# Rows of the split-weight buffers 1032 elements apart in place of 1024

## The chip, the cores and the metric

The kernel runs on one core of one Trainium2 chip. The metric is the device time of one execution, in microseconds (us). A time before of 1797.07 us is the median of three runs.

## What is computed

Two layers of an encoder block on 512 tokens of 1024 features, all in float32:

```
for l in range(2):
    x = x + 0.5 * swiglu(rms_norm(x, ffn1_norm[l]), ffn1_w_gate[l], ffn1_w_up[l], ffn1_w_down[l])
    p = rms_norm(x, mix_norm[l]) @ w_in[l]
    attn = mla_group(p[..., :672], ...)        # latent attention, 8 heads, chunk mask
    conv = conv_group(p[..., 672:], ...)       # gated causal depthwise convolution, 31 taps
    x = x + concatenate([attn, conv]) @ w_out[l]
    x = x + 0.5 * swiglu(rms_norm(x, ffn2_norm[l]), ffn2_w_gate[l], ffn2_w_up[l], ffn2_w_down[l])
    x = rms_norm(x, post_norm[l])

swiglu(x, g, u, d) = (silu(x @ g) * (x @ u)) @ d      # 1024 -> 2816 -> 1024
```

Nearly all of the arithmetic is in the matrix products with weights: four feed-forward blocks (two in each layer), the input projection and the output projection.

## The kernel before

**Split products.** Every float32 operand is split in two parts that TensorE takes in its float32r format: a high part, made by a cast on ScalarE, and a low part, the rest, made by a subtraction on VectorE. A product then is three (`mm3`, lines 170 to 172): high weights by high activations, high weights by low activations, low weights by high activations, all summed in PSUM. The weights are the stationary operand and the activations, features by tokens, the moving one.

**Weights.** A block of weights comes in by DMA as 128 rows of up to 1024 float32, into a tile `raw` (3 buffers) or, in the feed-forward blocks, also `fr` (4 buffers). `load_w` (lines 147 to 159) and `split_into` (lines 257 to 263) make the high part `wh` (line 151 or 260) and the low part `wl` (line 157 or 262). Each of `wh` and `wl` has 4 buffers, taken in turn, in the pool `w`. Some low parts are made by a DMA that adds the weights to their negated high part: into `ls` (`subtracted`, lines 405 and 406), or into `wl` for part of the output projection. A column block of 128 elements, 512 bytes in a row, is the stationary operand of one product.

**Activations.** The split activations lie in a ring `r` of 35 buffers of 512 elements, or, in the feed-forward blocks, also in `xj` (six buffers that hold high and low part side by side) and `xs`. In the mixing block between them some lie in `m`, a tile of a pool that is opened for that block.

**Feed-forward blocks.** The 22 column blocks of 128 hidden features are taken in pairs, in chunks (`CHUNKS`). The first two pairs of a block are computed plainly, with 512 columns (tokens) a product. For the others a fast scheme of seven block products in place of eight is used (`pair`), with operands combined by additions on VectorE. There the products have 256 columns, apart from those of `product_joined` (lines 389 and 390), where high and low activations of `xj` stream together as 512 columns against the high weights, and the high ones alone as 256 against the low weights. `down` does the same scheme for the middle chunks of the down projection, with 256 columns; the first and last chunk are computed plainly with 512.

**Order of the work.** The program is written in a fixed order and scheduled by a tool that orders each engine's instructions by priority and places tiles in memory. `issue_after` sets some orders by hand. Each pool is a stretch of memory whose tiles follow one another in the order in which their tags first appear:

```
cpool = ctx.enter_context(tc.tile_pool(name="const", bufs=1))
ring = ctx.enter_context(tc.tile_pool(name="ring", bufs=RING))
tmps = ctx.enter_context(tc.tile_pool(name="tmps", bufs=5))
wpool = ctx.enter_context(tc.tile_pool(name="w", bufs=4))
small = ctx.enter_context(tc.tile_pool(name="small", bufs=2))
```

In `w` the order is `raw`, `wh`, `wl`. The pools of the feed-forward and mixing blocks (`f`, with `fr`, `xj`, `xs`, `ls`; `k`, with `m`) are opened after `small` and lie behind it.

Of the kernel before, what the change touches and what calls it, by code (L numbers as in the profile page):

```python
# [7 lines left out]
FP = mybir.dt.float32  # L8
FR = mybir.dt.float32r
# [6 lines left out]
P = 128  # L16
# [15 lines left out]
NF = F // P  # L32
EPS = 1e-6
WC = 1024
HS = S // 2
RING = 35
WIDE = 6
# [41 lines left out]
def encoder_kernel(ctx: ExitStack, tc: tile.TileContext, xT, consts, vecs, rgain, wgu1, wd1, wdq1,  # L79
# [6 lines left out]
    wpool = ctx.enter_context(tc.tile_pool(name="w", bufs=4))  # L86
# [4 lines left out]
    def nm(s):  # L91
        uid[0] += 1
        return f"{s}{uid[0]}"
# [7 lines left out]
    def bank():  # L101
        return psum.tile([P, S], FP, tag="ps", name=nm("ps"))
# [44 lines left out]
    def load_w(src, w, kind=""):  # L147
        raw = wpool.tile([P, WC], FP, tag="raw", name=nm("raw"), bufs=3)
        nc.sync.dma_start(out=raw[:, :w], in_=src)
        hi = wpool.tile([P, WC], FR, tag="wh", name=nm("wh"))  # L150
        order["cast"] = A.copy(hi[:, :w], raw[:, :w]).ins  # L151
        lo = low()
        if kind == "sum":
            A.activation(lo[:, :w], raw[:, :w], AF.Copy, scale=-1.0)
            G.dma_start(out=lo[:, :w], in_=src, accum_op=ALU.add)
            return hi, lo
        (G if kind in POOLW.split() else V).tensor_tensor(lo[:, :w], raw[:, :w], hi[:, :w].bitcast(FP),  # L157
                                                          ALU.subtract)
        return hi, lo

    def low():
        return wpool.tile([P, WC], FR, tag="wl", name=nm("wl"))

    order = {}

# [3 lines left out]
    def mm3(o, lh, ll, rh, rl, first, last, free=False):  # L169
        T.matmul(o, lh, rh, start=first, stop=False, skip_group_check=free)  # L170
        T.matmul(o, lh, rl, start=False, stop=False, skip_group_check=free)  # L171
        order["mm"] = T.matmul(o, ll, rh, start=False, stop=last, skip_group_check=free).ins  # L172
        return order["mm"]
# [74 lines left out]
    def groups(srcs, rhs, ws=None):  # L248

        ws = ws or [load_w(src, WC) for src in srcs]  # L250
        os = [bank() for _ in srcs]
        for ks in (range(KD - 1), range(KD - 1, KD)):
            for o, w in zip(os, ws):
                group(o, w, rhs, ks, KD)
        return os

    def split_into(q, src, w=WC):

        hi = wpool.tile([P, WC], FR, tag="wh", name=nm("wh"))
        A.copy(hi[:, :w], src[:, :w])  # L260
        lo = low()
        order["lo"] = V.tensor_tensor(lo[:, :w], src[:, :w], hi[:, :w].bitcast(FP), ALU.subtract).ins  # L262
        return hi, lo
# [5 lines left out]
    def ffn_body(fpool, l, gx, norm, wgu, wd, wdq, gain, done, w0, halved):  # L269
# [52 lines left out]
        def operands(R):  # L322

            def joined(src):
                both = fpool.tile([P, 2, S], FR, tag="xj", name=nm("xj"), bufs=WIDE)
                A.copy(both[:, :, 0:HS], src)
                V.tensor_tensor(both[:, :, HS:S], src, both[:, :, 0:HS].bitcast(FP), ALU.subtract)
                return both
# [13 lines left out]
            for i in range(2):  # L342
                e, o = wide(quarter()), wide(quarter())
                for j in range(2):
                    for par, t in ((0, e), (1, o)):
                        m = 4 * i + 2 * j + par
                        V.scalar_tensor_tensor(t[:, j], x[:, m, :], gain[:, m:m + 1], R, ALU.mult, ALU.mult)
                        yield
                b11, b12, b21, b22 = (v[:, :, h * HS:(h + 1) * HS] for v in (e, o) for h in range(2))
                for n, src in (("b11", b11), ("b21", b21)):  # L350
# [21 lines left out]
        def product(o, w, n, start, stop):  # L372
            with tc.issue_after(order["pe"]):
                for gu in range(2):
                    for k in range(4):
                        hi, lo = X[n][k // 2]
                        t = slice(k % 2 * HS, (k % 2 + 1) * HS)
                        c = slice(gu * 512 + k * P, gu * 512 + (k + 1) * P)
                        last = mm3(o[:, gu * HS:(gu + 1) * HS], w[0][:, c], w[1][:, c], hi[:, t], lo[:, t],
                                   start and gu == 0 and k == 0, stop and k == 3, True)  # L380
            order["pe"] = last

        def product_joined(os, w, n, start):
            with tc.issue_after(order["pe"]):
                for gu, o in enumerate(os):
                    for k in range(4):
                        both = X[n][k // 2][:, k % 2]
                        c = slice(gu * 512 + k * P, gu * 512 + (k + 1) * P)
                        T.matmul(o, w[0][:, c], both, start=start and k == 0, stop=False, skip_group_check=True)  # L389
                        last = T.matmul(o[:, 0:HS], w[1][:, c], both[:, 0:HS], start=False, stop=k == 3,  # L390
                                        skip_group_check=True).ins
# [10 lines left out]
        def subtracted(w, src, n=WC):  # L402

            lo = fpool.tile([P, WC], FR, tag="ls", name=nm("ls"), bufs=2)
            A.activation(lo[:, :n], src[:, :n], AF.Copy, scale=-1.0)  # L405
            G.dma_start(out=lo[:, :n], in_=w, accum_op=ALU.add)  # L406
            return lo

        def summed(w, src, n=WC, lo=None):

            lo = subtracted(w, src, n) if lo is None else lo
            hi = wpool.tile([P, WC], FR, tag="wh", name=nm("wh"))
            A.copy(hi[:, :n], src[:, :n])
            return hi, lo

        def pair(p, quartered):

            a11, a12, a21, a22, s3 = quarters(wgu[l, p], WC, p == CHUNKS[0][1])
            bx, by, bz = bank(), (bank(), bank()), (bank(), bank())
            product(bx, split_into("a11", a11), "b11", True, True)  # L420
            a = copied(tmp(), bx)
            product_joined(by, summed(wgu[l, p, 1], a12), "b21", True)
            with after("first"):
                V.tensor_tensor(s3, a11, a21, ALU.add)
# [4 lines left out]
            for c, main, rest in parts(by):  # L429
                V.tensor_tensor(a[:, c], a[:, c], main, ALU.add)  # L430
                V.tensor_tensor(a[:, c], a[:, c], rest, ALU.add)
                if c.start == 0:
                    A.activation(s[:, 0:HS], a[:, 0:HS], AF.Silu)
            V.tensor_tensor(s[:, 0:HS], s[:, 0:HS], a[:, HS:S], ALU.mult)
            product(bx, split_into("s2", a11), "t2", False, True)
            r2 = wide(fpool.tile([P, WC], FP, tag="e", name=nm("e"), bufs=1))
            copied(r2[:, 0], bx)
            product_joined(bz, split_into("s3", s3), "t3", True)
            d = [copied(tmp(), o) for o in bz]
            for t in d:  # L440
# [3 lines left out]
            for t, (c, _, _) in zip(d, parts(bz)):  # L444
                order["first"] = V.tensor_tensor(r2[:, 1, c], t[:, 0:HS], r2[:, 1, c], ALU.subtract).ins
            product_joined(bz, summed(wgu[l, p, 3], a22), "t4", False)
            for c, main, rest in parts(bz):
                V.tensor_tensor(r2[:, 0, c], main, r2[:, 0, c], ALU.subtract)
# [89 lines left out]
        for p0, p1 in CHUNKS:  # L538
# [3 lines left out]
            for p in range(p0, p1):  # L542
                if p == 0:
                    os = []
                    for r in range(2):
                        ws = w0[2 * r:2 * r + 2] if w0 else [load_w(wgu[l, p, 2 * r + q], WC) for q in range(2)]
                        os.append([bank(), bank()])
                        if w0 and not r:
                            plain_first(os[r], ws)
                        elif w0:  # L550
                            plain(os[r][:1], ws, range(KD))
                            plain([None] + os[r][1:], ws, range(KD // 2))
                            with tc.issue_after(order["mm"]):
                                norm()
                            with after("sums"):
                                plain([None] + os[r][1:], ws, range(KD // 2, KD))
                        else:
                            plain(os[r], ws, range(KD - 1))
                            plain(os[r], ws, range(KD - 1, KD))
                            if not w0:  # L560
                                R = norm()
                    if not w0:
                        scaled(os, R)
                elif p < CHUNKS[0][1]:
                    for r in range(2):
                        ws = [load_w(wgu[l, p, 2 * r + q], WC) for q in range(2)]
                        o = [bank(), bank()]
                        if w0 and not r:
                            with tc.issue_after(order["mm"]):
                                plain(o[:1], ws, KS[:KD // 4])  # L570
                            with tc.issue_after(order["mm"]):
                                R = norm()
                            with after("spread"):
                                plain(o[:1], ws, KS[KD // 4:])
                                plain([None] + o[1:], ws, range(KD))
                            scaled(os, R)
                        else:
                            plain(o, ws, range(KD))
                        advance(8)
                        act.append(plain_out(o, R))  # L580
                else:
                    order.setdefault("pe", order["mm"])
                    act += pair(p, p0 > 0 and not last)
# [9 lines left out]
            for m in range(halved if last else KD):  # L593
                if m in ahead:
                    pd, w = ahead[m]
# [438 lines left out]
    class Finish:  # L1034
# [54 lines left out]
        def __call__(self):  # L1089
# [4 lines left out]
            for t in range(NT):  # L1094
# [8 lines left out]
    st = Stats()  # L1103
    f = gained(0, "g1", gx, first_gain)
    f(0)
    w0 = [tuple(wpool.tile([P, WC], t, tag=tag, name=nm(tag), bufs=n)
                for t, tag, n in ((FP, "raw", 3), (FR, "wh", 4), (FR, "wl", 4))) for _ in range(2)]

    def half_w(q, gu):
        raw, hi, lo = (v[:, gu * 512:(gu + 1) * 512] for v in w0[q])  # L1110
# [12 lines left out]
    w0 = [w[1:] for w in w0]  # L1123
# [172 lines left out]
```

## Time and profile before

| | |
|---|---|
| median of 3 runs | 1797.07 us (1794.69 to 1797.32) |
| the profiled execution | 1794.2 us |
| its span in the trace | 1792.4 us |
| TensorE products busy | 1778.5 us (99%) |
| TensorE weight loads busy | 1579.1 us (88%) |
| VectorE busy | 1493.5 us (83%) |
| ScalarE busy | 1093.8 us (61%) |
| GpSimd busy | 382.1 us (21%) |
| moved by DMA | 228.28 MB, 127 GB/s in the mean |

In the profile, PE is TensorE's matrix products and PEld its loads of stationary operands, which run beside the products; DVE is VectorE, ACT ScalarE, POOL GpSimd, SP the engine that issues most DMAs. A row of a grouped view names the line, the engine, the operation, the tile written, the tiles read, the shape and the count; after the bar stand the busy time, the mean duration in ns and the engine's idle time before such instructions, with what ended it. Products are pipelined, so the mean duration of one is longer than the time from its start to the next one's. A row of the timeline begins with start and duration in us.

### The profile page before, as it was taken

What the parts mean: (1) busy time and instruction counts of PE and PEld (TensorE: products, weight loads), DVE (VectorE), ACT (ScalarE), POOL (GpSimd) and SP (SyncE); (2) the same over time, 40 slices, a digit from 0 to 9 for tenths busy, and PEclk for the clock granted to TensorE, in tenths of its full rate; (3) what the DMA queues carried; (4) which work ended last, traced back from release to release, by engine and by line L of the source; (5) the groups of instructions that cost most, each with busy time, mean ns of one, the idle gap of its engine ahead of it and who ended that gap; (6) DMA issues with size and microseconds to landing.
All of it is one profiled execution on the core that took longest, in us unless ns stands there. A gap on an engine that the chain in (4) does not pass through costs nothing.

```text
span 1792.4 us, 29441 instructions
## 1 busy us (share of the span) xinstructions
PE 1778.5 (99%) x11430; PEld 1579.1 (88%) x11430; DVE 1493.5 (83%) x2309; ACT 1093.8 (61%) x1699; POOL 382.1 (21%) x313
## 2 busy tenths in 40 slices
PE   9999999999999999999999999999999999999998
PEld 7899999888678899999888999998976788999997
DVE  7898988689965989898779989876999568989883
ACT  5565756467853575756645757564778435756564
POOL 1000000248722000000310000002585310000002
PEclk9999999999999999999999999999999999999999
DMA  5657575324213466665426575743260126575742
GB/s 170 171 131 182 136 178 123 109 84 127 68 28 96 124 166 162 153 160 131 124 65 171 123 194 122 193 114 111 81 157 21 52 79 170 130 185 131 183 117 74
DMA packets 71947, 228.28 MB, mean 127 GB/s; under 512 B 8448, under 2 KB 9600, under 8 KB 71808
## 3 DMA queue, kind: packets, MB, share of 16 engines
q1 hardware_dynamic: 55536, 171.87, 30.5%
q0 software_dynamic: 16128, 54.53, 18.2%
q8 instruction: 89, 1.46, 0.3%
q14 instruction: 50, 0.41, 0.1%
q10 hardware_dynamic: 144, 0.00, 0.0%
HBM read 222.19 MB, written 2.10 MB: 125 GB/s over the span
## 4 chain that ended last, share of the span: by engine, by line
PE 90%; DVE 6%; ACT 1%; issue 1%; DMA 1%; POOL 0%; SPq 0%; ACTq 0%; DVEq 0%
PE ps L170 24%; PE ps L171 23%; PE ps L172 23%; PE ps L389 11%; PE ps L390 6%; DVE cv L968 1%; DVE mx L876 1%; DMA raw<-in_wgu 1%; PE ps L917 1%; DVE r L898 0%; PE ps L895 0%; PE ps L214 0%; DVE r L855 0%; PE ps L676 0%; DVE wl L262 0%
## 5 line engine op out<-in xcount | busy, mean ns | idle before, releaser
L171 PE MATMUL ps<-r,wh 128*128 128x256 f32 (+1 forms) x2556 | 812.9, 319 | 0.1
L170 PE MATMUL ps<-r,wh 128*128 128x256 f32 (+1 forms) x2556 | 811.0, 320 | 1.1 <-ACT wh L151 0.5
L172 PE MATMUL ps<-r,wl 128*128 128x256 f32 (+1 forms) x2364 | 755.3, 321 | 0.0
L170 PEld LDWEIGHTS ps<-r,wh 128*128 128x128 f32 x2556 | 483.8, 189 | 45.6 <-ACT wh L151 3.7
L171 PEld LDWEIGHTS ps<-r,wh 128*128 128x128 f32 x2556 | 484.6, 190 | 36.4 <-DVE r L178 1.5
L172 PEld LDWEIGHTS ps<-r,wl 128*128 128x128 f32 x2364 | 448.2, 190 | 33.8
L389 PE MATMUL ps<-xj,wh 128*128 128x512 f32 x864 | 303.8, 391 | 0.0
L151 ACT CAST wh<-raw 128x1024 fp32r<-128x1024 f32 (+3 forms) x148 | 132.6, 901 | 216.9 <-PE ps L171 135.3
L260 ACT CAST wh<-fr 128x1024 fp32r<-128x1024 f32 (+1 forms) x160 | 157.8, 986 | 103.8 <-DVE fr L426 49.3
L406 POOL DMA_DIRECT2D ls<-in_wgu x72 | 62.5, 868 | 734.5 <-ACT ls L405 525.0
L157 DVE TENSOR_TENSOR wl<-raw,wh 128x1024 fp32r<-128x1024 f32 (+3 forms) x132 | 141.2, 1077 | 91.0 <-ACT wh L151 90.3
L262 DVE TENSOR_TENSOR wl<-fr,wh 128x1024 fp32r<-128x1024 f32 (+1 forms) x160 | 181.8, 1136 | 20.1 <-ACT wh L260 20.1
L389 PEld LDWEIGHTS ps<-xj,wh 128*128 128x128 f32 x864 | 161.4, 188 | 30.1
L390 PE MATMUL ps<-xj,ls 128*128 128x256 f32 x576 | 161.3, 280 | 0.0
L974 POOL TENSOR_TENSOR y<-y,pr 128x495 f32<-128x495 f32 (+29 forms) x90 | 121.7, 1353 | 46.4 <-ACT pr L972 41.0
L260 ACT CAST wh<-raw 128x1024 fp32r<-128x1024 f32 (+1 forms) x100 | 98.1, 981 | 45.2 <-PE ps L171 24.5
L262 DVE TENSOR_TENSOR wl<-raw,wh 128x1024 fp32r<-128x1024 f32 (+1 forms) x100 | 113.3, 1133 | 14.2 <-ACT wh L260 13.8
L390 PEld LDWEIGHTS ps<-xj,ls 128*128 128x128 f32 x576 | 108.3, 188 | 0.0
L405 ACT ACTIVATE ls<-fr 128x1024 fp32r<-128x1024 f32 (+1 forms) x56 | 56.1, 1002 | 75.9 <-PE ps L390 42.8
L207 POOL TENSOR_TENSOR r<-r,t 128x512 f32<-128x512 f32 x45 | 73.3, 1638 | 136.5 <-ACT t L203 136.2
L968 DVE SCALAR_TENSOR_TENSOR cv<-m,vec,cv 128x511 f32<-128x511 f32 (+14 forms) x120 | 87.8, 732 | 3.8 <-ACT cv L964 2.2
L406 POOL DMA_DIRECT2D ls<-in_wdq x32 | 27.6, 863 | 262.1 <-ACT ls L405 262.1
(257 smaller groups left out, 2919.1 us busy)
## 6 DMA issues: line engine op xcount, KB each, us to landing
fr<-in_wgu SPq DMA_DIRECT2D x112, 512.0 KB, 4.3
ls<-in_wgu POOLq DMA_DIRECT2D x72, 512.0 KB, 6.3
raw<-in_wgu SPq DMA_DIRECT2D x62, 512.0 KB, 4.6
fr<-in_wdq SPq DMA_DIRECT2D x48, 384.0 KB, 5.0
ls<-in_wdq POOLq DMA_DIRECT2D x32, 384.0 KB, 4.8
raw<-in_wd SPq DMA_DIRECT2D x32, 384.0 KB, 3.2
raw<-in_wd SPq DMA_DIRECT2D x32, 256.0 KB, 2.8
raw<-in_wcv SPq DMA_DIRECT2D x16, 512.0 KB, 3.6
```

The costliest lines, as they stand in the source:

```text
L151: order["cast"] = A.copy(hi[:, :w], raw[:, :w]).ins
L157: (G if kind in POOLW.split() else V).tensor_tensor(lo[:, :w], raw[:, :w], hi[:, :w].bitcast(FP), ALU.subtract)
L170: T.matmul(o, lh, rh, start=first, stop=False, skip_group_check=free)
L171: T.matmul(o, lh, rl, start=False, stop=False, skip_group_check=free)
L172: order["mm"] = T.matmul(o, ll, rh, start=False, stop=last, skip_group_check=free).ins
L260: A.copy(hi[:, :w], src[:, :w])
L262: order["lo"] = V.tensor_tensor(lo[:, :w], src[:, :w], hi[:, :w].bitcast(FP), ALU.subtract).ins
L389: T.matmul(o, w[0][:, c], both, start=start and k == 0, stop=False, skip_group_check=True)
L390: last = T.matmul(o[:, 0:HS], w[1][:, c], both[:, 0:HS], start=False, stop=k == 3, skip_group_check=True).ins
L406: G.dma_start(out=lo[:, :n], in_=w, accum_op=ALU.add)
L968: V.scalar_tensor_tensor(acc[:, s:], u[c][:, :S - s], tap(k), acc[:, s:], ALU.mult, ALU.add)
L974: order["conv"] = G.tensor_tensor(ys[c][:, s:], ys[c][:, s:], pr[:, s:], ALU.add).ins
```

## The change

The rows of all `wh` and `wl` tiles are 1032 elements (4128 bytes) apart in place of 1024 (4096 bytes). The same elements of them are written and read; the last 8 of a row are left unused. Buffer k of four then begins 32 k bytes further than before within its kind, the `wl` buffers as a whole 128 bytes further, and what lies behind them 256 bytes further. The `raw` tiles keep rows of 1024.

```
@@ -32,6 +32,7 @@
 WC = 1024
+WP = WC + 8
@@ load_w
-        hi = wpool.tile([P, WC], FR, tag="wh", name=nm("wh"))
+        hi = wpool.tile([P, WP], FR, tag="wh", name=nm("wh"))
@@ low
-        return wpool.tile([P, WC], FR, tag="wl", name=nm("wl"))
+        return wpool.tile([P, WP], FR, tag="wl", name=nm("wl"))
@@ split_into
-        hi = wpool.tile([P, WC], FR, tag="wh", name=nm("wh"))
+        hi = wpool.tile([P, WP], FR, tag="wh", name=nm("wh"))
@@ summed
-            hi = wpool.tile([P, WC], FR, tag="wh", name=nm("wh"))
+            hi = wpool.tile([P, WP], FR, tag="wh", name=nm("wh"))
@@ the first weights of the kernel
-    w0 = [tuple(wpool.tile([P, WC], t, tag=tag, name=nm(tag), bufs=n)
-                for t, tag, n in ((FP, "raw", 3), (FR, "wh", 4), (FR, "wl", 4))) for _ in range(2)]
+    w0 = [tuple(wpool.tile([P, w], t, tag=tag, name=nm(tag), bufs=n)
+                for t, tag, n, w in ((FP, "raw", 3, WC), (FR, "wh", 4, WP), (FR, "wl", 4, WP))) for _ in range(2)]
```

## The prediction

> **What bounds the kernel now.** I read the page first, then the busy time by stage, then the matrix products grouped by shape, then the timeline of TensorE alone.
>
> ```profile
> span 1792.4 us, 29441 instructions
> PE 1778.5 (99%) x11430; PEld 1579.1 (88%) x11430; DVE 1493.5 (83%) x2309; ACT 1093.8 (61%) x1699; POOL 382.1 (21%) x313
> PEclk9999999999999999999999999999999999999999
> PE 90%; DVE 6%; ACT 1%; issue 1%; DMA 1%; POOL 0%; SPq 0%; ACTq 0%; DVEq 0%
> ```
>
> TensorE is busy 1778.5 of 1792.4 us, at full clock, and carries 90% of the chain that ended last. The busy time by stage (columns: length, then busy time and instruction count of each engine) says that this holds in every large stage:
>
> ```profile
> 75.00:310.00 235.00, 234.84 (x1764) 225.05 (x1764) 208.84 (x323) 154.11 (x213) 20.71 (x24) 1.00 0.61 152
> 520.00:600.00 80.00, 80.00 (x356) 65.80 (x355) 49.08 (x64) 33.31 (x49) 21.92 (x11) 1.00 0.28 83
> 1407.00:1500.00 93.00, 93.00 (x412) 76.18 (x411) 61.66 (x86) 40.91 (x60) 23.16 (x13) 1.00 0.34 99
> ```
>
> So a time that the change adds to or takes from one matrix product is paid in full, and what it does to VectorE, ScalarE or a DMA is hidden unless TensorE comes to wait for it. These are the products, by moving tile, stationary tile and columns:
>
> ```profile
> L170 PE MATMUL ps<-r,wh 128*128 128x256 f32 x1704 | 482.9, 283 | 0.6
> L171 PE MATMUL ps<-r,wh 128*128 128x256 f32 x1704 | 482.1, 283 | 0.0
> L172 PE MATMUL ps<-r,wl 128*128 128x256 f32 x1512 | 427.6, 283 | 0.0
> L171 PE MATMUL ps<-r,wh 128*128 128x512 f32 x852 | 331.1, 390 | 0.1
> L172 PE MATMUL ps<-r,wl 128*128 128x512 f32 x852 | 328.2, 390 | 0.0
> L170 PE MATMUL ps<-r,wh 128*128 128x512 f32 x852 | 328.1, 395 | 0.5 <-ACT wh L151 0.5
> L390 PE MATMUL ps<-xj,ls 128*128 128x256 f32 x576 | 161.3, 280 | 0.0
> L390 PE MATMUL ps<-xj,wl 128*128 128x256 f32 x288 | 78.2, 281 | 0.0
> ```
>
> The mean there (283 or 390 ns) is the life of one pipelined product. What the end of the kernel feels is the step from one start to the next, which only the timeline shows. While one product streams, the stationary tile of the next is read, so each step has two reads of SBUF side by side: the moving tile and the next weights.
>
> **Where the tiles lie now.** This follows from the pools in the code. Ring (35 rows of 2048 bytes), temporaries (5 of 2048), raw (3 of 4096), wh and wl (4 of 4096 each) follow one another, all multiples of 1024 bytes, so every r tile, every wh and every wl slot has the same offset modulo 512, and the column blocks of 512 bytes inside them keep it. The small pool then adds 5,152 bytes (its rows rounded up to 32), five times 1024 and 32 more. So the tiles of the pools opened after it (m, xj, xs, ls, fr) lie 32 bytes off the r, wh and wl tiles. The kernel of before therefore already holds both cases, moving tile and weights at one offset, and 32 bytes apart. TensorE's timeline for 512 columns, start in us first:
>
> ```profile
> 527.13 0.39 PE L170 MATMUL ps<-r,wh 128*128 128x512 f32 x1
> ...
> 530.30 0.39 PE L172 MATMUL ps<-r,wl 128*128 128x512 f32 x1
> 530.53 0.40 PE L170 MATMUL ps<-m,wh 128*128 128x512 f32 x1
> ...
> 531.69 0.40 PE L170 MATMUL ps<-r,wh 128*128 128x512 f32 x1
> ...
> 533.08 0.40 PE L170 MATMUL ps<-r,wh 128*128 128x512 f32 x1
> ```
>
> From 527.13 to 530.30 are 14 steps with r against wh and wl at one offset: 3.17 us, 226.4 ns each. From 530.53 to 531.69 the moving tile is m, 32 bytes off: 5 steps in 1.16 us, 232.0 ns. The 6 steps behind them, r again, take 1.39 us, 231.7 ns: the stream has left its rhythm and takes a while to find it. All 11 together: 2.55 us, 231.8 ns, which is 5.4 ns (2.4%) over the even streak. For 256 columns:
>
> ```profile
> 95.10 0.28 PE L172 MATMUL ps<-r,wl 128*128 128x256 f32 x1
> ...
> 97.26 0.28 PE L172 MATMUL ps<-r,wl 128*128 128x256 f32 x1
> ```
> ```profile
> 92.37 0.28 PE L170 MATMUL ps<-xs,wh 128*128 128x256 f32 x1
> ...
> 93.08 0.28 PE L170 MATMUL ps<-r,wh 128*128 128x256 f32 x1
> ```
> ```profile
> 145.95 0.28 PE L172 MATMUL ps<-r,ls 128*128 128x256 f32 x1
> ...
> 147.72 0.28 PE L172 MATMUL ps<-r,ls 128*128 128x256 f32 x1
> ```
>
> Here the sign is the other one. At one offset (r against wh, wl) 18 steps take 2.16 us, 120.0 ns. With xs as the moving tile, 32 bytes off, 6 steps take 0.71 us, 118.3 ns; with ls as the low part of the weights, off the other way, 15 steps take 1.77 us, 118.0 ns. So the even offset is a good case for 512 columns and a poor one for 256.
>
> **The change part by part.** It adds and removes no instruction, wait or DMA: every wh and wl tile gets rows of 4128 bytes in place of 4096, and only 1024 elements of each are used. The wh and wl slots then lie 0, 32, 64 and 96 bytes further than now (modulo 128); r stays; the pools behind move by 256 bytes and keep their 32.
>
> *Products of 512 columns on r.* 3 times 852 are 2556 steps. The slots are taken in turn, so in three steps of four the weights are off the r tiles: 1917 steps. At 5.4 ns more each: +10.4 us. That puts the offsets of 64 and 96 at the price of 32, which is the only row there is. Below, the lot costs nothing, if a stream at any constant offset finds an even rhythm of 226.4; above, all 2556 pay, since the even steps behind an uneven one did (231.7): +13.8 us. I take +10.4, as both measured stretches, m and r behind m, stand at 232.
>
> *Products of 256 columns on r against wh and wl.* 3 times 1512 are 4536 steps, 3402 of them uneven after the change; at 118.3 in place of 120.0 that is 1.7 ns less each, -5.8 us. Not all of it arrives: streaks are short here, some steps are below 120 already behind a change of tile, and VectorE, 208.84 of 235 us busy in such a stage, makes the low parts and then ends some waits later. The ends are 0 and -5.8; I take -4.
>
> *Joined products* (L389 with 512 columns and L390 with 256, moving xj). Two timelines, eight pairs on wl and five on ls:
>
> ```profile
> 83.24 0.40 PE L389 MATMUL ps<-xj,wh 128*128 128x512 f32 x1
> ...
> 86.02 0.28 PE L170 MATMUL ps<-r,wh 128*128 128x256 f32 x1
> ```
> ```profile
> 89.93 0.39 PE L389 MATMUL ps<-xj,wh 128*128 128x512 f32 x1
> ...
> 91.65 0.28 PE L170 MATMUL ps<-r,wh 128*128 128x256 f32 x1
> ```
>
> With wl (32 off xj) a pair takes 2.78/8 = 347.5 ns; with ls (same offset as xj) 1.72/5 = 344.0. The 288 wl pairs can gain at most 3.5 ns each where a slot comes to lie even with xj, -1.0 us; the 576 ls pairs keep ls and see only wh move, at worst the same 3.5 ns: +2.0 us. I take 0.
>
> *Casts and subtractions.* They write wh and wl, and read wh.
>
> ```profile
> L262 DVE TENSOR_TENSOR wl<-fr,wh 128x1024 fp32r<-128x1024 f32 x112 | 136.3, 1217 | 20.1 <-ACT wh L260 20.1
> L262 DVE TENSOR_TENSOR wl<-raw,wh 128x1024 fp32r<-128x1024 f32 x68 | 82.8, 1217 | 10.8 <-ACT wh L260 10.8
> L260 ACT CAST wh<-fr 128x1024 fp32r<-128x1024 f32 x112 | 117.7, 1051 | 74.3 <-DVE fr L426 49.3 <-PE ps L171 13.6 <-PE ps L389 7.7
> L260 ACT CAST wh<-raw 128x1024 fp32r<-128x1024 f32 x68 | 71.4, 1050 | 21.8 <-PE ps L171 21.8
> ```
>
> fr lies 32 bytes off wh and wl, raw lies even with them, and the means agree, 1217 with 1217 and 1051 with 1050. The offset costs these engines nothing, so the operands come when they came. No DMA writes wh, and the few that add into wl write the same runs of 4096 bytes.
>
> Sum: +10.4 - 4 + 0 = +6.4 us. The profiled execution took 1794.2 us (span 1792.4 and 1.8 around it) and gives 1800.6; the median of the runs is 1797.07, 2.9 above it, and gives 1803.5. I forecast 1803.
>
> A rule of the Trainium skill speaks for no effect at all. Its page "SBUF — State Buffer", section "Who interferes with whom", says that TensorE has two independent read ports, one for the moving operand and one for loading weights, and that "PE and ACT never wait on anyone". By it the sum would be 0. The trace does not agree as far as the two reads of TensorE itself go: 226.4 against 232.0 ns, with nothing changed but the moving tile.
>
> **The rivals.** *Faster.* A stream of 512 columns at a constant uneven offset settles too, after its first steps, and costs nothing; the 256-column products keep their gain: -5.8 us, 1791.3. For it speaks that the m streak is only 5 steps long, so what I priced may be the change of offset rather than the offset; against it, that high and low slots differ, so the offset alternates within every three products. It decides where an uneven 512 step costs under 5.8/1917 = 3.0 ns. Chance 0.14.
>
> *No change.* The slow steps around m belong to the change of tile alone, or the gain and the loss cancel, or the rows are placed on coarser steps than 32 bytes so that the offsets do not arise: 0 us, 1797. Against it stand all three uneven streaks, each different from its even one. Chance 0.15.
>
> *Much slower.* No 512-column stream keeps its rhythm any more, even steps included (+13.8), and the 256-column ones give nothing back, because other offsets than 32 are as slow as the even one: 1810.9, with +2.0 from the ls pairs 1812.9. For it speaks that r behind m stayed at 231.7 for six steps. Chance 0.16.
>
> *My forecast* has 0.55; its own range is 1799 (a third of the 512 cost) to 1807 (all of it, little given back).
>
> **How the numbers follow.** Measurement tells about 0.2%, 3.6 us, from no change. The forecast lies 6 us above, a small part of its range within 3.6; so slower 0.68 (0.16 and nearly all of 0.55), same 0.17, faster 0.15. The range goes from the faster rival's 1791 to the much slower one's 1813.
>
> **What would show it.** Right: the same instructions in the same order; PE busy up by about what the span is up; in stages with 512 columns (520 to 600, 1407 to 1500) steps of 229 to 234 in place of 226.4 and longer stages; in stages with 256 columns steps of 118 to 119 and stages as long or shorter; L260 and L262 at 1051 and 1217. Wrong: steps of 226.4 in the 512-column stages; or time in the 256-column stages lost to waits for wh and wl; or another order of instructions.

## The result and the profile after

The changed kernel takes 1802.54 us (median of 7 runs, 1801.09 to 1806.22) against 1797.07 for the kernel before; the ratio is 1.0035, 95% interval 1.0024 to 1.0045. It is slower by about 6 us. The instructions are the same 29441, and the order of the products, of their weight loads and of the instructions on ScalarE and GpSimd is that of before (on VectorE one pair that starts 1 ns apart in the trace stands the other way round); only addresses differ. The line numbers of the changed kernel are one higher from line 35 on.

The head of its page, and its busy time by stage, in the same stretches as before:

```profile
span 1799.5 us, 29441 instructions
PE 1785.8 (99%) x11430; PEld 1574.4 (87%) x11430; DVE 1493.6 (83%) x2309; ACT 1094.4 (61%) x1699; POOL 381.3 (21%) x313
```
```profile
75.00:310.00 235.00, 234.76 (x1773) 224.06 (x1772) 209.59 (x325) 154.60 (x213) 20.71 (x24) 1.00 0.62 153
520.00:600.00 80.00, 80.00 (x349) 64.69 (x348) 47.54 (x62) 31.35 (x45) 21.94 (x11) 1.00 0.27 82
1407.00:1500.00 93.00, 93.00 (x405) 75.18 (x404) 59.05 (x80) 41.72 (x62) 21.96 (x11) 1.00 0.26 79
```

The span is up by 7.1 us and PE's busy time by 7.3. In the two stages of 512 columns 349 products fit where 356 did, and 405 where 412 did; in the stage of mostly 256 columns 1773 fit where 1764 did. So one kind of product became slower and the other faster, as forecast.

The steps show it directly. Two stretches of unbroken r products that both kernels have, one of 180 steps of 512 columns and one of 203 of 256 (first product, and the product after the last). TensorE's timeline before:

```profile
862.45 0.40 PE L172 MATMUL ps<-r,wl 128*128 128x512 f32 x1
...
903.29 0.39 PE L172 MATMUL ps<-r,wl 128*128 128x512 f32 x1
```
```profile
779.16 0.28 PE L171 MATMUL ps<-r,wh 128*128 128x256 f32 x1
...
803.43 0.40 PE L389 MATMUL ps<-xj,wh 128*128 128x512 f32 x1
```

and after:

```profile
864.22 0.39 PE L173 MATMUL ps<-r,wl 128*128 128x512 f32 x1
...
905.99 0.39 PE L173 MATMUL ps<-r,wl 128*128 128x512 f32 x1
```
```profile
781.16 0.28 PE L172 MATMUL ps<-r,wh 128*128 128x256 f32 x1
...
805.15 0.40 PE L390 MATMUL ps<-xj,wh 128*128 128x512 f32 x1
```

512 columns: 40.84 us for 180 steps before, 226.9 ns each; 41.77 after, 232.1 ns. 256 columns: 24.27 us for 203 steps, 119.6 ns; 23.99 after, 118.2 ns.

Summed over the trace, from each start to the next, the r products against wh and wl come to (the 18 and 3 steps that a product without split weights follows are left out): 512 columns 582.6 us before, 594.3 after (+11.7); 256 columns 592.7 and 586.4 (-6.3); all else +1.7. That is the 7.1 us of the span. In these sums a step that waited counts too. Without the steps longer than 253 ns (512 columns) or 147 ns (256 columns), the mean step went from 227.2 to 231.7 and from 119.5 to 118.0. The table below gives this mean.

The casts and subtractions, by form, take what they took (1217, 1217, 1051 and 1050 ns before):

```profile
L263 DVE TENSOR_TENSOR wl<-fr,wh 128x1024 fp32r<-128x1024 f32 x112 | 136.4, 1218 | 20.3 <-ACT wh L261 20.3
L263 DVE TENSOR_TENSOR wl<-raw,wh 128x1024 fp32r<-128x1024 f32 x68 | 82.8, 1218 | 10.3 <-ACT wh L261 10.3
L261 ACT CAST wh<-fr 128x1024 fp32r<-128x1024 f32 x112 | 117.5, 1049 | 75.7 <-DVE fr L427 52.6 <-PE ps L172 15.1 <-PE ps L390 8.0
L261 ACT CAST wh<-raw 128x1024 fp32r<-128x1024 f32 x68 | 71.2, 1047 | 20.9 <-PE ps L172 20.9
```

### The profile page after: what moved, and what is told of

It reads as the page before. It is cut to its first block, busy times and chain, and to the rows that moved or that the text cites. A ratio compares the mean times of both kernels' runs of the same rounds, so it can differ in the third digit from the quotient of the medians.

```text
span 1799.5 us, 29441 instructions
## 1 busy us (share of the span) xinstructions
PE 1785.8 (99%) x11430; PEld 1574.4 (87%) x11430; DVE 1493.6 (83%) x2309; ACT 1094.4 (61%) x1699; POOL 381.3 (21%) x313
## 4 chain that ended last, share of the span: by engine, by line
PE 55%; DVE 4%; ACT 1%; issue 0%; DMA 0%; ACTq 0%; DVEq 0%
PE ps L171 14%; PE ps L173 14%; PE ps L172 14%; PE ps L390 7%; PE ps L391 4%; DVE cv L969 1%; DVE mx L877 0%; DVE wl L263 0%; PE ps L918 0%; DMA fr<-in_wdq 0%; DVE r L179 0%; DVE r L899 0%; PE ps L215 0%; PE ps L896 0%; ACT pr L973 0%
## 5 line engine op out<-in xcount | busy, mean ns | idle before, releaser
L152 ACT CAST wh<-raw 128x1024 fp32r<-128x1024 f32 (+3 forms) x148 | 132.3, 899 | 228.8 <-PE ps L172 152.5
```

## The experiments

The theory of the prediction (the offset): the step depends on the distance in memory between the moving tile and the weights read beside it. Its rival (the rhythm): only the change of distance from product to product costs, and a stream at any constant distance settles at 226.4 ns. All kernels below have the products of before in the same order. Each ratio is against runs of the kernel before on the same chip, made beside it; their medians were 1795.79 to 1796.57 us.

**One constant distance for all weights.** The kernel of before with some bytes ahead of the pool `w`, so that every wh and wl slot lies the same distance from r. The pools behind move along.

```
-    wpool = ctx.enter_context(tc.tile_pool(name="w", bufs=4))
+    ctx.enter_context(tc.tile_pool(name="shim", bufs=1)).tile([P, 8], FP, tag="shim", name="shim")   # 8: 32 bytes
+    wpool = ctx.enter_context(tc.tile_pool(name="w", bufs=4))
```

> The kernel of before with 32 unused bytes ahead of the pool w: all wh and wl slots lie 32 bytes off the r tiles, constantly, and the pools behind (m, xj, xs, ls) keep their 32 to wh and wl. Theory of the offset (an uneven offset by itself makes a 512-column step 232 ns and a 256-column step 118): 2556 x 5.4 = +13.8 us and 4536 x -1.7 = -7.7 us, sum +6.1, about 1803 us against 1797. Theory of the rhythm (only the change of offset from product to product costs, a constant one settles): 512-column steps at 226 to 227 ns, 256-column steps at 118 to 120, sum 0 to -7.7, 1789 to 1797 us.

> As shift32 with 64 bytes. Theory of the offset: as in shift32 if 64 is as uneven as 32 (+6.1 us, 1803), or as before if the chip tells only 64-byte runs apart (0, 1797). Theory of the rhythm: 512-column steps settle at 226 to 227 ns again, sum 0 to -7.7, 1789 to 1797 us.

> As shift32 with 96 bytes. Theory of the offset: +6.1 us, 1803. Theory of the rhythm: 0 to -7.7 us, 1789 to 1797. If steps depend on the sign of the distance, shift32 and shift96 part by more than 4 us.

> As shift32 with 128 bytes. If the distance counts modulo 128 (as the reckoning with four slots at 0, 32, 64 and 96 bytes takes it), both theories expect the kernel of before: 512-column steps 226 to 227 ns, 256-column steps 120, 1797 us. If it counts modulo more, the steps are those of an uneven offset: 1803 by the theory of the offset.

Four more distances followed, 192 and 256 first, 160 and 224 after them.

> As shift64 with 192 bytes ahead of the pool w. By a price for each distance: another pair of steady steps. If only the distance modulo 128 counted, those of shift64: 233 ns (512 columns) and 113 to 115 ns (256), 1796 us; shift128 against before speaks against that, and then 512 columns at 227 to 234 ns and 256 at 113 to 120, 1784 to 1808 us. The kernel is worth having where 512 columns stay at 227 and 256 columns come to 113.

> As shift64 with 256 bytes. If the distance counts modulo 256: the kernel of before, 227 and 120 ns, 1796 us. If modulo 512: another pair of steps, 1784 to 1808 us.

> As shift64 with 160 bytes, a distance that the wl slots of the changed kernel have. No theory gives its step beforehand: 227 to 234 ns (512 columns) and 113 to 120 (256), 1784 to 1808 us. With it, shift224 and the six others the price of all eight distances modulo 256 is known, and the mean over the slots of the changed kernel (wh 0 to 96, wl 128 to 224) can be held against its measured 231.7 and 118.0 ns.

> As shift160 with 224 bytes: 227 to 234 ns and 113 to 120 ns, 1784 to 1808 us.

| distance, bytes | 512-column step, ns | 256-column step, ns | time against before (95%) |
|---|---|---|---|
| 0 (before) | 227.2 | 119.5 | 1 |
| 32 | 233.3 | 118.4 | 1.0045 (1.0032 to 1.0058) |
| 64 | 233.3 | 115.3 | 0.9992 (0.9983 to 1.0000) |
| 96 | 234.2 | 118.7 | 1.0066 (1.0053 to 1.0078) |
| 128 | 232.5 | 118.9 | 1.0051 (1.0037 to 1.0065) |
| 160 | 233.4 | 119.8 | 1.0076 (1.0064 to 1.0089) |
| 192 | 229.1 | 116.7 | 0.9977 (0.9968 to 0.9985) |
| 224 | 233.4 | 116.9 | 1.0015 (1.0006 to 1.0023) |
| 256 | 227.3 | 119.5 | 0.9999 (0.9990 to 1.0008) |

The rival falls. At a constant 32 bytes the same 180 steps stay slow to their end, 41.99 us, 233.3 ns each:

```profile
865.82 0.40 PE L172 MATMUL ps<-r,wl 128*128 128x512 f32 x1
...
907.81 0.40 PE L172 MATMUL ps<-r,wl 128*128 128x512 f32 x1
```

And the distance counts modulo 256, not 128, as I had taken it: shift128 is 0.5% slower than before, and shift256 is the kernel of before again, 40.84 us for the 180 steps (864.36 to 905.20), 226.9 ns:

```profile
864.36 0.40 PE L172 MATMUL ps<-r,wl 128*128 128x512 f32 x1
...
905.20 0.39 PE L172 MATMUL ps<-r,wl 128*128 128x512 f32 x1
```

The direction counts too: 192 bytes, which modulo 256 is 64 the other way, leaves the 512-column step at 229.1 ns, where 64 has 233.3.

The shim moves the weights' own place in memory as well as their distance from r. The products on xj tell the two apart, since xj moves along with the weights and keeps its distance: their 512-column steps stay between 228.4 and 230.4 ns at all the distances of the table, where those on r go from 227.2 to 234.2. So it is the distance that counts, not the place.

With 64 bytes the two kinds of product go furthest apart. The timeline of shift64 for the 180 steps of 512 columns, for the 203 of 256 columns, and for another stretch of 203 like it:

```profile
861.27 0.39 PE L172 MATMUL ps<-r,wl 128*128 128x512 f32 x1
...
903.27 0.40 PE L172 MATMUL ps<-r,wl 128*128 128x512 f32 x1
```
```profile
779.56 0.28 PE L171 MATMUL ps<-r,wh 128*128 128x256 f32 x1
...
802.92 0.39 PE L389 MATMUL ps<-xj,wh 128*128 128x512 f32 x1
```
```profile
690.45 0.28 PE L171 MATMUL ps<-r,wh 128*128 128x256 f32 x1
...
714.36 0.39 PE L389 MATMUL ps<-xj,wh 128*128 128x512 f32 x1
```

233.3 ns for 512 columns; for 256 columns 115.1 in one stretch and 117.8 in the other. The products and the distance are alike, so at this distance a stream settles at one of two rhythms. The triples of a product show them: most take 340 ns (113, 113, 114) or 353 to 354. The same two come at 192 bytes, there with more triples at 353 to 354. What picks one is open.

**The change on one kind of tile.**

```
-        return wpool.tile([P, WC], FR, tag="wl", name=nm("wl"))
+        return wpool.tile([P, WC + 8], FR, tag="wl", name=nm("wl"))
```

(and the same in the first weights of the kernel; for wh_rows_only the three places of wh in its stead)

> The change on the wl tiles alone: rows of 1032 elements for wl, 1024 for wh. Two of three products then read wh at the offset of r, as before, and one of three reads wl at 0, 32, 64 or 96 bytes. If each step is priced by the weights that are read during it: 512-column steps stay at 227 ns in two of three and go to 232 in one, 852 x 5 = +4 us, 256-column ones gain 1.6 ns in one of three, 1500 x 1.6 = -2.4 us; sum +2, about 1798 us. If one uneven read spoils the steps that follow it: all 2556 steps of 512 columns near 231 to 232 (+11 to +13 us), the 256-column ones 118 (-6), sum +5 to +7, about 1802 us.

wl_rows_only: 1800.22 us, 1.0029 (1.0021 to 1.0038); 512-column steps 231.0 ns in the mean. In two of three steps there the weights read beside the product are wh, at the even distance, and by a price for each read the mean would be (2 x 227.2 + 232.0)/3 = 228.8, with 232.0 the mean of 0 to 96 bytes in the table. The stretch of 180 steps, 41.50 us, 230.6 ns:

```profile
864.05 0.40 PE L172 MATMUL ps<-r,wl 128*128 128x512 f32 x1
...
905.55 0.40 PE L172 MATMUL ps<-r,wl 128*128 128x512 f32 x1
```

So an uneven read does spoil the steps after it: the steps with the even wh beside them have means of 230.6 and 230.7 ns, not 227.2. A price for each read and the lost rhythm agree where all slots are uneven, and part here.

The rhythm is not lost for long. The 96 steps from 420.58 us on belong to four weight tiles. In one of them, as many as have an even wl, 21 steps in a row take 4.76 us, about 227 ns each. The other three have means of 233.0, 232.3 and 231.5 ns, and in them the steps with the even wh beside them are at 229.5 to 233.0 as well.

```profile
426.86 0.39 PE L170 MATMUL ps<-r,wh 128*128 128x512 f32 x1
...
431.62 0.39 PE L170 MATMUL ps<-r,wh 128*128 128x512 f32 x1
```

So an uneven read spoils the steps of its own tile, and a tile with even reads soon finds the even step again. (That this tile is the one with the even wl is inferred, since the trace does not name the buffer.)

> The change on the wh tiles alone: rows of 1032 elements for wh, 1024 for wl, which as a whole moves by 128 bytes. If the parts add up: the whole change cost 6.3 us and wl alone 5.2, so about +1 us, 1797 us. If one uneven read spoils the rhythm of all, and the constant distance of 128 counts as in shift128: 2556 steps of 512 columns near 232 (+13) and 4536 of 256 columns near 118.5 (-5), sum +6 to +8, 1802 to 1804 us.

wh_rows_only: 1801.32 us, 1.0029 (1.0018 to 1.0040), steps 231.7 and 118.7 ns. It does not add up (5.2 us for wl, about as much for wh, about 6 for both). It is not a clean half, since wl as a whole moves by 128 bytes, an uneven distance of its own. At +5 us it lies a little under the 6 to 8 expected of a spoiled rhythm.

**A better version.** The table asks for 512-column products at distance 0 and 256-column products at 64, 192 or 224. In the fast down projection the rows have room. The edit, shortened (`summed` has `n` in place of `w`):

```
 split_into, summed (only rows of 768):
-        hi = wpool.tile([P, WC], FR, tag="wh", name=nm("wh"))
+        hi = wpool.tile([P, WC], FR, tag="wh", name=nm("wh"))[:, 16 * (w < WC):]
-        lo = low()
+        lo = low()[:, 16 * (w < WC):]
 subtracted:
-            lo = fpool.tile([P, WC], FR, tag="ls", name=nm("ls"), bufs=2)
+            lo = fpool.tile([P, WC], FR, tag="ls", name=nm("ls"), bufs=2)[:, 8 * (n < WC):]
```

> The kernel of before, with the weights of the fast down projection alone (768 of the 1024 elements of a row are used there, moving tiles r, 256 columns) written 16 elements (64 bytes) further into their wh and wl tiles, and 8 elements further into ls, which lies 32 bytes off already. The 512-column products keep the even offset. If the steady step belongs to the distance alone, as in shift64: 672 triples of products at 340 in place of 356 to 360 ns, -10.8 to -13.4 us; some of it is lost where VectorE and ScalarE make the operands too late, so -6 to -13 us, 1783 to 1790 us. If shift64's 113 ns came from the whole layout: no change, 1796 us.

down64: 1792.74 us, 0.9983 (0.9975 to 0.9992). The gain of 3 us is real, and less than the 6 to 13 that I expected. The r products of 256 columns together went from 592.7 to 589.7 us. Most of those in the down projection settled at the slower of the two rhythms, 23.96 us for the 203 steps, 118.0 ns, where the kernel before had 119.6; and the steps that waited lost 7.6 us in place of 5.0.

```profile
779.83 0.28 PE L171 MATMUL ps<-r,wh 128*128 128x256 f32 x1
...
803.79 0.40 PE L389 MATMUL ps<-xj,wh 128*128 128x512 f32 x1
```

> shift192, with the weights of the plain down projection (512 or 768 of the 1024 elements of a row) written 16 elements, 64 bytes, further into their wh and wl tiles, so that they lie 256 bytes from r. If the distance counts modulo 256: their 308 triples of 512-column products go from 687 to 680 ns, -2.1 us, and the 24 triples of 256 columns among them from 352 to 360, +0.2: 1789.4 us against shift192's 1791.3. If not: 1791 us or more.

shift192 itself was already faster than both kernels, 1791.34 us, 0.9977 (0.9968 to 0.9985): 41.20 us for the 180 steps (228.9 ns) and 23.90 for the 203 (117.7 ns).

```profile
861.44 0.39 PE L172 MATMUL ps<-r,wl 128*128 128x512 f32 x1
...
902.64 0.39 PE L172 MATMUL ps<-r,wl 128*128 128x512 f32 x1
```
```profile
779.00 0.28 PE L171 MATMUL ps<-r,wh 128*128 128x256 f32 x1
...
802.90 0.40 PE L389 MATMUL ps<-xj,wh 128*128 128x512 f32 x1
```

shift192_down writes the weights of `load_w` for the plain down projection 16 elements further in their rows (the same slice as in down64). It took 1791.07 us, 0.9967 (0.9954 to 0.9979), the fastest of the kernels here. Its 512-column steps fell from 229.1 to 228.4 ns in the mean, 1.6 us over the 2497 steps counted; the two intervals overlap, so the last step is seen in the trace and not in the times.

## Why the prediction was right

*The offset is the mechanism.* Shown by the shift kernels: the same instructions in the same order, and with the weights and the pools behind them moved away from r, gave 0.9977 to 1.0076 of the time; the products on xj, whose distance to the weights stayed, kept their step to about 1 ns.

*Products of 512 columns: forecast +10.4 us, measured +11.7.* The price for an uneven step was near (5.4 ns; the table has 5 to 7 for all distances but 192, which has 1.9). The count was wrong, and for a reason: I took the distance modulo 128, so that the wl tiles, which move by a further 128 bytes as a whole, had a slot even with r. Modulo 256 wl has none, and wh one in four. Since even steps among uneven ones are spoiled too, the mean over all steps rises by 4.5 ns: 2538 x 4.5 = 11.4, against 1917 x 5.4 = 10.4. Too few steps at too high a price: two errors that nearly cancel, which is luck.

*Products of 256 columns: forecast -4, measured -6.3, under my end of -5.8.* The mean gain came to 1.5 ns where I had 1.7, but by luck: the only distance that I had read, 32 bytes, gives 1.1 over a whole trace (shift32), 160 gives nothing, and 64, 192 and 224 give 2.6 to 4.2. The count was too low. I took three quarters of 4536 steps, and the 4536 leave out 384 high-weight products whose low part is ls; the 1.5 is the mean over all the steps counted, 4917 x 1.5 = 7.4. Only about 1 us of it was lost in longer waits, where I had taken off a third.

*The mean over the slots.* wh lies 0, 32, 64 and 96 bytes off, wl 128, 160, 192 and 224. The means of the table are 232.0 and 232.1 ns for 512 columns and 118.0 and 118.1 for 256. Measured were 231.7 and 118.0. The change comes out as an average over eight distances: it gives up the best distance for 512 columns and leaves the next-to-worst for 256. That wl_rows_only does not follow such an average, read by read, shows its limit.

*Joined products: forecast 0, measured +2.5 us, over my end of +2.0.* I had the ls pairs unchanged but for wh. The first half of each pair became slower:

```profile
L390 PE MATMUL ps<-xj,wh 128*128 128x512 f32 x864 | 306.3, 395 | 0.0
```

against 303.8 us and 391 ns before. Its steps, 512 columns on xj, went from 229.5 to 232.8 ns in the mean, +2.9 us, and the second half gave 0.4 back. A pair with ls took 350.6 ns in the mean in place of 346.8, 3.8 more, where I had 3.5 at worst. That ls kept its distance to xj did not save it, which fits the spoiled rhythm of wl_rows_only but was not tested by itself.

*Casts and subtractions: forecast 0, measured 0*, as the rows above show.

*The sum.* Forecast +6.4 us, measured +7.1 in the span. The 512-column term was 1.3 us short, the 256-column term gave 2.3 more than I took, the joined products cost 2.5 that I had at 0, and the rest gave 0.8 back. The mechanism held; that the time came within 1 us of 1803 owes something to these errors cancelling.

*The rivals.* Faster by settling: fell with shift32. No change: fell with the interval of the result; shift256 adds that a move by itself changes nothing. The Trainium skill, page "SBUF — State Buffer", section "Who interferes with whom", says that TensorE never waits on anyone; the runs here differ by 1% with the distance of TensorE's own two reads, so on this point the measurement decides. What in the memory makes the two reads meet is not shown by any run.

*Much slower* was right that even steps are spoiled as well, and wrong in that the 256-column products gave nothing back.

## What to carry to other kernels

Where TensorE is the bound and each step streams a moving tile while it loads the next weights, the distance of the two tiles in memory can count. For the float32r products here, modulo 256 bytes, it is worth up to 3% of a 512-column step (234.2 against 227.2 ns) and 4% of a 256-column one (119.8 against 115.3), and the best distance for the one is not that for the other. Spreading buffers over several offsets averages the cases; finding the one distance that suits the mix of products is better: a dummy tile of 192 bytes made this kernel faster (0.9977), where the padding of every row made it slower (1.0035). Before a change of addresses is judged by its few measured neighbours, the modulus has to be measured too.

## What the runs showed of the hardware

Beyond the modulus of 256 bytes and the two rhythms at 64 and 192, one thing came unasked. In the profile of the changed kernel the granted clock fell for a short time at 1402 us; the busy time by stage after, then before:

```profile
1402.00:1407.00 5.00, 5.00 (x14) 3.47 (x13) 0.91 (x2) 1.49 (x2) 0.70 (x1) 0.66 0.00 0
```
```profile
1402.00:1407.00 5.00, 5.00 (x24) 4.10 (x23) 3.45 (x6) 4.20 (x8) 0.00 (x0) 1.00 0.00 0
```

The trace's record of the granted clock has half speed for 3.41 us from 1402.74 on; a mean of 0.66 over 5 us gives the same, 0.34 x 5 / 0.5 = 3.4 us. It costs 1.7 us at most, an estimate. It stands behind the end of the mixing block, where products wait for the statistics of the convolution. The Trainium skill, page "TensorE: Matmul & The Clock Gate", Part 1, gives a free-running window of 3413 ns in which TensorE's activity is judged; the length agrees. The profile of before has no such dip there, those of shift192 and shift256 have one each, and one more elsewhere (at 508 and at 7 us). So the 7.1 us between the two spans hold up to 1.7 us that one profile has and another of the same kernel may not; the stretches and mean steps above are free of it. The sum for 512 columns is not: six of its steps fall into the dip, at 415 to 427 ns, about 1.2 us.
